# Layer 0 projects the raw x: the norm's gain moves into the weight split, its root into the results

## The chip, the cores and the metric

The kernel runs on one core of one Trainium2 chip. A time is the device time of one launch in microseconds (us); a kernel is timed several times and its median is compared. A profile is one further look at one execution: its span runs from the first to the last recorded instruction.

## The reference

Four residual layers, then a last RMSNorm, for 256 tokens of width 1024 in float32. Layer 0 and layer 3 are pooling layers, layer 1 is a gated DeltaNet, layer 2 an attention. Only the start of layer 0 and its pooling mixer matter here:

```python
def rmsnorm(x, g):
    y = xf * lax.rsqrt(jnp.mean(xf * xf, axis=-1, keepdims=True) + EPS)
    return (y * g.astype(jnp.float32)).astype(x.dtype)

def pool_mixer(h, w_in, w_grp, scale, w_out):        # h = rmsnorm(x, norm_g[0])
    u, gate = jnp.split(h @ w_in, 2, axis=-1)        # 1024 -> 2 x 2048
    ...                                              # windowed means of u, minus u, per group of 512
    p = jnp.einsum('bsgi,gio->bsgo', p, w_grp).reshape(B, S, POOL_WIDTH)
    y = p * scale * jax.nn.silu(gate)
    return y @ w_out
```

## The kernel before

Tokens lie in two tiles of 128 (`xs[0]`, `xs[1]`, 1024 columns each). A projection contracts over `k`, eight blocks of 128 channels (`KD`), into strips of 512 output columns (`CW`). Each float32 product is made of three matmuls on operands split in two parts, `hi` (rounded for TensorE) and `lo` (the rest): hi·hi, hi·lo, lo·hi. So every weight block of 128x512 that lands in a `raw` tile is split by `weights`: ScalarE writes `whi` (line 117), VectorE writes `wlo = raw - whi` (line 119). Nine such pairs can be held (`ring`, 9 buffers); a pair's buffers come free when the matmuls that read them have ended.

The normed input goes in as `hT`: the four 128x128 blocks of half a token tile are transposed on TensorE into a PSUM bank (`tp`, line 324), then split by ScalarE and VectorE (`split_out`, lines 196 and 201) into `hTh` and `hTl`.

The work of layer 0 in order: for the four groups `g` = 3, 2, 1, 0 a `gate` strip and a `pooled` strip (each 1024 x 512), with the group's own 512x512 product (`mixed`) one group behind; then `layer_out`. The first gate strip (`rows`, line 168) puts tokens on the output's partitions, 48 matmuls with 512 columns: 8 blocks x 2 token tiles x 3. The other seven strips (`chan=True`, lines 127 to 129) put channels on the partitions, 96 matmuls with 256 columns each. A gate strip's result is turned by ScalarE through Silu (line 421), a pooled strip's copied by ScalarE (line 429).

The start, before the change: both halves of `xs[0]` are loaded, the gain `norm_g[0]` is loaded as a tile broadcast over all 128 partitions (`gain_tile`, line 277), `part_done` takes the mean square of the rows (ScalarE, line 210), GpSimd its root (line 297), VectorE writes the normed `h` (line 304), and only then `h` is transposed. Loads of the second token tile stand behind those of four weight blocks. Meanwhile 24 transposes of the identity (line 271) are issued to TensorE, with no use for their result.

The order of instructions on each engine comes from a scheduler that runs over the whole program when it is built; `later(...)` holds instructions back behind named ones. All loads of x and of weights are issued by SyncE (SP) in one queue. Each engine runs its own instructions in order and waits by semaphores.

Of the kernel before, what the change touches and what calls it, by code (L numbers as in the profile page):

```python
# [8 lines left out]
F32 = mybir.dt.float32  # L9
# [3 lines left out]
AF = mybir.ActivationFunctionType  # L13
# [29 lines left out]
def trunk(ctx: ExitStack, tc: tile.TileContext, x, positions, norm_g, pool_w_in, pool_w_grp,  # L43
# [6 lines left out]
    WARM = 24  # L50
    FREE = 4
    EARLY = 6
    E0 = 2
    E1 = 4
# [27 lines left out]
    def bank(pool, name):  # L82
        return pool.tile([P, CW], F32, tag=name, name=name)
# [13 lines left out]
    def weights(src, n, cols, raw=None, pool=()):  # L97
# [12 lines left out]
        for k in range(n):  # L110
            v = raw[:, k * cols:(k + 1) * cols]
            lo = ring.tile([P, CW], F32R, tag="wlo", name="wlo")[:, :cols]
            hi = ring.tile([P, CW], F32R, tag="whi", name="whi")[:, :cols]
            held = held_back["free"] <= 0
            held_back["free"] -= 1
            with later(*(held_back["after"] if held else ())):
                a = nc.scalar.copy(hi, v)  # L117
                e = nc.gpsimd if k in pool else nc.vector
                b = e.tensor_tensor(out=lo, in0=v, in1=hi.bitcast(F32), op=ALU.subtract)  # L119
            parts.append((hi, lo))  # L120
# [10 lines left out]
    def project(src, ks, act, cols=CW, chan=False, tail=0, done=None, cuts=1,  # L131
                where="acc", pool=()):
# [9 lines left out]
        def unit(k0, n):  # L142
            return weights(src(k0, n), n, cols,
                           pool=[a for a in range(n) if (k0 + a) % KD in pool])
# [44 lines left out]
    def units(n):  # L189
        return [(k, KU) for k in range(0, n, KU)]  # L190
# [63 lines left out]
    def load_x(t):  # L254
        for c in range(2):
            sl = slice(c * CW, (c + 1) * CW)
            nc.sync.dma_start(out=xs[t][:, sl], in_=x[0, t * P:(t + 1) * P, sl])

    load_x(0)
# [9 lines left out]
    ps = bank(tps, "tp")  # L269
    for _ in range(WARM):  # L270
        nc.tensor.transpose(ps[:, :P], ident, ident)

    def gain_tile(row, between):
# [6 lines left out]
        return g  # L280

# [130 lines left out]
    def pool_layer(i, j, hT):  # L412
        yT = Split("yT", POOL_W // P)
        order = (3, 2, 1, 0)

        def gate(g):
            ks = [(k, 1) for k in range(KD)] if g == order[0] and i == 0 else units(KD)
            banks = project(cols_of(pool_w_in[j], POOL_W + g * CW), ks, hT, chan=g != order[0])
            gs = [worka("gs", CW) for _ in range(NT)]
            for t in range(NT):  # L420
                nc.scalar.activation(gs[t], banks[t], AF.Silu)
            return gs

        def pooled(g):
            w = WINDOWS[g]
            banks = project(cols_of(pool_w_in[j], g * CW), units(KD), hT, chan=True)
            u = big("u", 4, S)
            for b in range(2):
                nc.scalar.copy(u[:, 2 * b:2 * b + 2, :],  # L429
                               banks[b].rearrange("p (c s) -> p c s", c=2))  # L430
# [784 lines left out]
    def prefetch(k, pool=()):  # L1215
        ready.append(weights(first(k, 1), 1, CW, worka("raw", CW), pool))

    def start(t):
        with later(*held_back["after"], *[mark[e] for e in ("act", "dve") if t]):
            for a in range(0, D, CW):  # L1220
                part_done(t, a, CW, apart=True)
            for a in range(0, D, CW):
                if t:
                    nxt.begin(t, a)
            nxt.feed(t)

    held_back["free"] = 100
    nxt = LayerIn(0, lambda: prefetch(0, (0,)))
    for k in range(1, E0):
        prefetch(k)  # L1230
    start(0)
    held_back["free"] = 0
    for k in range(max(1, E0), E1):
        prefetch(k)
    load_x(1)
    start(1)
    for k in range(E1, EARLY):
        prefetch(k)
# [33 lines left out]
```

## Time and profile before

| what | value |
|---|---|
| median of 3 timed runs | 859.24 us (858.56, 859.24, 861.16) |
| span of the profiled execution | 858.3 us |
| time of the profiled execution outside of its span | not given; the timed runs lie 0.3 to 2.9 us above the span |
| granted TensorE clock, mean | 0.988 |
| TensorE busy, matmuls | 836.9 us (98%) |
| VectorE busy | 594.2 us (69%) |
| ScalarE busy | 490.2 us (57%) |
| TensorE busy, 0 to 18.57 us | 11.52 us |
| TensorE busy, 18.57 to 171 us (the rest of layer 0) | 152.43 us of 152.43 |

In a row of the timeline stand the start and the duration in us, the engine, the line, the operation, the tiles (written from read) and how often; the brackets at the end tell how long the engine had idled, and what ended it. In a row of the windows stand the stretch and its length, then for PE (matmuls), PEld (weight loads), DVE (VectorE), ACT (ScalarE) and POOL (GpSimd) the busy us and the instructions, then the clock granted to TensorE as a share of full speed, the busy share of the DMA engines and the GB/s they moved. A row of the groups gives line, engine, operation, tiles, shapes and count, then busy us and mean ns of one, then the idle time before. Matmuls are pipelined: the distance of their starts, not the duration of one, is what a stream of them costs.

### The profile page before, as it was taken

The numbers are of one execution on the slowest core, as the hardware profiler recorded it, in microseconds if no ns is written. First come the engines' busy times: TensorE is split into PE (matmuls) and PEld (weight loads), VectorE is DVE, ScalarE is ACT, GpSimd is POOL, SyncE is SP. The second block draws the span as 40 slices with busy tenths as digits, with TensorE's granted clock in tenths as the row PEclk, the third lists the DMA queues.
The fourth block names the chain that finished last, engine by engine and source line by source line (L and its number), as shares of the span: only waits on it lengthen the run. The fifth ranks groups of instructions, "written<-read, shape, count | busy, mean of one in ns | idle before, by whom it ended". The sixth has DMA issues, their size and how long they took to land.

```text
span 858.3 us, 16132 instructions
## 1 busy us (share of the span) xinstructions
PE 836.9 (98%) x5967; PEld 778.9 (91%) x5967; DVE 594.2 (69%) x1140; ACT 490.2 (57%) x1007; POOL 155.2 (18%) x295
## 2 busy tenths in 40 slices
PE   6999999999999989999999999999999999999996
PEld 5999998988999988788979998999989989999986
DVE  4689866556988976355577659678767668867852
ACT  5566564467855744355465654566555475555642
POOL 4000000233237980022212002000000210000012
PEclk8999999999999999899999999999999999999999
DMA  6766666646655554123547676743552546556551
GB/s 196 245 190 185 179 194 198 194 138 198 193 141 168 171 149 131 66 67 106 173 139 217 198 171 172 195 127 97 172 163 82 175 148 209 182 179 196 190 201 50
DMA packets 109239, 140.42 MB, mean 164 GB/s; under 512 B 21228, under 2 KB 51112, under 8 KB 109160
## 3 DMA queue, kind: packets, MB, share of 16 engines
q1 hardware_dynamic: 106800, 137.65, 53.1%
q0 software_dynamic: 528, 1.58, 0.7%
q8 instruction: 47, 0.77, 0.4%
q10 hardware_dynamic: 1832, 0.16, 0.2%
q14 instruction: 32, 0.26, 0.1%
HBM read 137.79 MB, written 1.58 MB: 162 GB/s over the span
## 4 chain that ended last, share of the span: by engine, by line
PE 82%; POOL 7%; DVE 5%; DMA 3%; issue 2%; ACT 1%; SPq 0%; POOLq 0%; ACTq 0%; DVEq 0%
PE acc L168 33%; PE acc L128 11%; PE acc L127 11%; PE acc L129 11%; POOL Tb L732 3%; POOL pr L728 2%; PE aux L127 2%; PE aux L128 2%; PE aux L129 2%; DVE wlo L119 1%; DMA gain<-in_norm_g_dram 1%; DVE cv L637 1%; DVE h L304 1%; PE aux L861 1%; DMA Gb<-d_g 1%
## 5 line engine op out<-in xcount | busy, mean ns | idle before, releaser
L119 DVE TENSOR_TENSOR wlo<-raw,whi 128x512 fp32r<-128x512 f32 (+1 forms) x493 | 342.5, 717 | 162.6 <-ACT whi L117 155.4
L117 ACT CAST whi<-raw 128x512 fp32r<-128x512 f32 (+1 forms) x508 | 301.8, 617 | 256.7 <-PE acc L168 100.4
L127 PE MATMUL acc<-hTh,whi 128*128 128x256 f32 x832 | 234.3, 282 | 1.2 <-DVE vc L637 1.2
L128 PE MATMUL acc<-hTl,whi 128*128 128x256 f32 x832 | 235.0, 283 | 0.0
L129 PE MATMUL acc<-hTh,wlo 128*128 128x256 f32 x832 | 233.8, 281 | 0.0
L127 PEld LDWEIGHTS acc<-hTh,whi 128*128 128x128 f32 x832 | 156.9, 189 | 1.8 <-DVE vc L637 1.4
L128 PEld LDWEIGHTS acc<-hTl,whi 128*128 128x128 f32 x832 | 156.9, 189 | 0.4
L129 PEld LDWEIGHTS acc<-hTh,wlo 128*128 128x128 f32 x832 | 156.8, 189 | 0.2
L168 PE MATMUL acc<-wlo,yTh 128*128 128x256 f32 (+1 forms) x384 | 116.5, 319 | 0.0
L168 PE MATMUL acc<-whi,yTh 128*128 128x256 f32 (+1 forms) x384 | 116.4, 323 | 0.0
L168 PE MATMUL acc<-whi,yTl 128*128 128x256 f32 (+1 forms) x384 | 92.7, 322 | 0.0
L168 PEld LDWEIGHTS acc<-wlo,yTh 128*128 128x128 f32 x384 | 72.1, 188 | 5.1
L168 PEld LDWEIGHTS acc<-whi,yTh 128*128 128x128 f32 x384 | 71.7, 188 | 5.2
L168 PEld LDWEIGHTS acc<-whi,yTl 128*128 128x128 f32 x384 | 63.2, 188 | 5.5
L292 POOL TENSOR_TENSOR hg<-x,gain 128x256 f32<-128x256 f32 x18 | 14.9, 834 | 259.1 <-DVE x L354 257.4
L168 PE MATMUL acc<-wlo,hTh 128*128 128x512 f32 (+1 forms) x144 | 56.3, 396 | 0.4 <-DVE wlo L119 0.2
L168 PE MATMUL acc<-whi,hTh 128*128 128x512 f32 (+1 forms) x144 | 55.6, 394 | 0.7 <-ACT hTh L196 0.7
L168 PE MATMUL acc<-whi,hTl 128*128 128x512 f32 (+1 forms) x144 | 45.7, 389 | 0.0
L435 POOL COPY win<-u 128x4 f32<-128x4 f32 x8 | 2.8, 355 | 177.2 <-ACT u L429 177.2
L168 PEld LDWEIGHTS acc<-whi,hTh 128*128 128x128 f32 x144 | 27.5, 191 | 6.8 <-ACT hTh L196 1.7
L168 PEld LDWEIGHTS acc<-wlo,hTh 128*128 128x128 f32 x144 | 27.3, 190 | 6.8 <-DVE wlo L119 1.7
L168 PEld LDWEIGHTS acc<-whi,hTl 128*128 128x128 f32 x144 | 26.8, 190 | 5.5
(339 smaller groups left out, 1444.5 us busy)
## 6 DMA issues: line engine op xcount, KB each, us to landing
raw<-in_pool_w_in_dram SPq DMA_DIRECT2D x60, 512.0 KB, 4.5
raw<-in_gdn_w_in_dram SPq DMA_DIRECT2D x48, 512.0 KB, 3.9
raw<-in_pool_w_out_dram SPq DMA_DIRECT2D x32, 512.0 KB, 4.2
raw<-in_mla_w_in_dram SPq DMA_DIRECT2D x24, 512.0 KB, 4.6
raw<-in_mla_w_uq_dram SPq DMA_DIRECT2D x36, 256.0 KB, 3.4
raw<-in_pool_w_grp_dram SPq DMA_DIRECT2D x16, 512.0 KB, 4.1
raw<-in_gdn_w_out_dram SPq DMA_DIRECT2D x16, 512.0 KB, 3.7
raw<-in_mla_w_ukv_dram SPq DMA_DIRECT2D x32, 256.0 KB, 3.3
```

What stands on the lines that cost most here:

```text
L117: a = nc.scalar.copy(hi, v)
L119: b = e.tensor_tensor(out=lo, in0=v, in1=hi.bitcast(F32), op=ALU.subtract)
L127: nc.tensor.matmul(o, lhsT=lhs[0], rhs=rhs[0], start=start, stop=False)
L128: nc.tensor.matmul(o, lhsT=lhs[0], rhs=rhs[1], start=False, stop=False)
L129: return nc.tensor.matmul(o, lhsT=lhs[1], rhs=rhs[0], start=False, stop=stop)
L168: nc.tensor.matmul(o, lhsT=act(k, t * P, P)[x], rhs=parts[j][z][:, sl], start=k == first and x == z == 0, stop=k == last and x == 1)
L292: nc.gpsimd.tensor_tensor(out=self.early[t, a], in0=xs[t][:, sl], in1=self.g[:, sl], op=ALU.mult)
L304: nc.vector.scalar_tensor_tensor(out=h[:, cut:], in0=xs[t][:, sl], scalar=r[:, 0:1], in1=self.g[:, sl], op0=ALU.mult, op1=ALU.mult)
L637: nc.vector.scalar_tensor_tensor(out=o[:, d:], in0=ps[:, :S - d], scalar=tp(3 - d, c), in1=o[:, d:], op0=ALU.mult, op1=ALU.add)
L728: nc.gpsimd.tensor_tensor(out=pv, op=ALU.mult, in0=Lb[:, r, r + 1:, None].to_broadcast([M * Q, n, c]), in1=Tb[:, r:r + 1, :c].to_broadcast ...
L732: mark["blocks"] = nc.gpsimd.tensor_tensor(out=tv, in0=tv, in1=pv, op=ALU.subtract).ins
L861: nc.tensor.matmul(ps[:, c], lhsT=U[0][:, h, :], rhs=vR[h // 2][:, 0, c * DV:(c + 1) * DV], start=True, stop=True)
```

## The change

Layer 0 no longer forms a normed `h`. It transposes and splits x itself, half a token tile at a time, as it lands (`First.feed`). The gain `norm_g[0]` is loaded as 8 rows of 128 by ScalarE's queue (`grow`), transposed to columns (`First.columns`), and multiplied into every weight block of layer 0's input projection when it is split: ScalarE's `hi` is now an activation with a per-partition scale, VectorE's `lo` a scalar_tensor_tensor. The root of the mean square is applied to the results: in the first gate strip as the per-partition scale of the Silu, in the other seven strips by a VectorE multiply with `rT`, the roots spread over all partitions (`First.scales`: two matmuls of a diagonal with ones, and a copy). There the ScalarE copy of a pooled strip is gone, and the Silu of a gate strip follows the multiply. Loads of x and weights alternate. Of TensorE's idle work, 5 and 2 matmuls of ones are left in place of the 24 transposes. Layers 1 to 3 and the last norm are as before.

```diff
-    WARM = 24
+    WARM = (5, 2)
...
+                if gain is None:
+                    a = nc.scalar.copy(hi, v)
+                    b = e.tensor_tensor(out=lo, in0=v, in1=hi.bitcast(F32), op=ALU.subtract)
+                else:
+                    g = gain[:, k:k + 1]
+                    a = nc.scalar.activation(hi, v, AF.Copy, scale=g)
+                    b = e.scalar_tensor_tensor(out=lo, in0=v, scalar=g, in1=hi.bitcast(F32),
+                                               op0=ALU.mult, op1=ALU.subtract)
...
-    load_x(0)
+    load_x(0, 0)
+    grow = small("grow", P, bufs=1)[:KD]
+    nc.scalar.dma_start(out=grow, in_=norm_g[0].rearrange("(k p) -> k p", p=P))
+    ones = const.tile([P, P], F32, name="ones")
+    nc.vector.memset(ones, 1.0)
...
-    ps = bank(tps, "tp")
-    for _ in range(WARM):
-        nc.tensor.transpose(ps[:, :P], ident, ident)
+
+    def warming(n):
+        ps = bank(tps, "tp")
+        for _ in range(n):
+            nc.tensor.matmul(ps[:, :P], lhsT=ones, rhs=ones, start=True, stop=True)
+
+    warming(WARM[0])
...
+    class First:
...
+        def columns(self):
+            ps = bank(tps, "tp")
+            nc.tensor.transpose(ps[:, :KD], grow, ident[:KD, :KD])
+            nc.vector.tensor_copy(self.gain, ps[:, :KD])
+
+        def feed(self, t, c):
+            ps = bank(tps, "tp")
+            for b in range(4):
+                a = c * CW + b * P
+                nc.tensor.transpose(ps[:, b * P:(b + 1) * P], xs[t][:, a:a + P], ident)
+            return split_out((ps.rearrange("p (b s) -> p b s", b=4),
+                              self.hT.many(4 * c, 4, t * P, P), None))
+
+        def scales(self):
+            ps = bank(aux, "aux")
+            for t in range(NT):
+                nc.gpsimd.tensor_tensor(out=self.r[t], in0=ms[t], in1=neghalf[:, :1], op=ALU.pow)
+                d = workb("diag", P)
+                nc.vector.tensor_scalar(d, ident, self.r[t], None, ALU.mult)
+                nc.tensor.matmul(ps[:, t * P:(t + 1) * P], lhsT=ones, rhs=d, start=True, stop=True)
+            nc.vector.tensor_copy(self.rT, ps[:, :S])
...
+        def scaled(o, ps):
+            nc.vector.tensor_tensor(
+                out=o, in0=ps.rearrange("p (c s) -> p c s", c=2), op=ALU.mult,
+                in1=lead.rT[:, None, :].to_broadcast([P, 2, S]))
...
-            for t in range(NT):
-                nc.scalar.activation(gs[t], banks[t], AF.Silu)
+            if lead and not chan:
+                lead.scales()
+            for t in range(NT):
+                if not lead:
+                    nc.scalar.activation(gs[t], banks[t], AF.Silu)
+                elif chan:
+                    scaled(gs[t].rearrange("p (c s) -> p c s", c=2), banks[t])
+                    nc.scalar.activation(gs[t], gs[t], AF.Silu)
+                else:
+                    nc.scalar.activation(gs[t], banks[t], AF.Silu, scale=lead.r[t])
...
             for b in range(2):
-                nc.scalar.copy(u[:, 2 * b:2 * b + 2, :],
-                               banks[b].rearrange("p (c s) -> p c s", c=2))
+                if lead:
+                    scaled(u[:, 2 * b:2 * b + 2, :], banks[b])
+                else:
+                    nc.scalar.copy(u[:, 2 * b:2 * b + 2, :],
+                                   banks[b].rearrange("p (c s) -> p c s", c=2))
...
+    nxt = First()
+    nxt.columns()
+    turn = nxt.feed(0, 0)
+    with later(*turn):
+        prefetch(0)
+        warming(WARM[1])
+        prefetch(1)
+    load_x(1, 0)
+    with later(mark["act"], mark["dve"]):
+        turn = nxt.feed(1, 0)
+    with later(*turn):
+        prefetch(2)
+        prefetch(3)
+        part_done(0, 0, CW, apart=True)
+    load_x(0, 1)
+    load_x(1, 1)
...
```

What moves is seen in the order in which the built programs hold their instructions. SyncE's queue at the start of the program, before (`x_93` and `x_94` are the two token tiles, `raw` the weight blocks):

```order
L257 DMA x_93<-in_x_dram 128x512 x2
L277 DMA gain<-in_norm_g_dram 128x512
L104 DMA raw<-in_pool_w_in_dram 128x512
L277 DMA gain<-in_norm_g_dram 128x512
L104 DMA raw<-in_pool_w_in_dram 128x512 x3
L257 DMA x_94<-in_x_dram 128x512 x2
```

and now:

```order
L260 DMA x_93<-in_x_dram 128x512
L101 DMA raw<-in_pool_w_in_dram 128x512
L260 DMA x_94<-in_x_dram 128x512
L101 DMA raw<-in_pool_w_in_dram 128x512
L260 DMA x_93<-in_x_dram 128x512
L101 DMA raw<-in_pool_w_in_dram 128x512
L260 DMA x_94<-in_x_dram 128x512
L101 DMA raw<-in_pool_w_in_dram 128x512
```

The two broadcast loads of the gain are gone from this queue, and the second token tile's first half stands third in place of eighth.

TensorE at the start of the program, before (`tp` are the transposes' banks, `acc` the sums of a strip):

```order
L271 MATMUL tp<-ident 128x128 x24
L324 MATMUL tp<-ident,h 128x128 x8
L168 MATMUL acc<-whi,hTh_168 128x512
L168 MATMUL acc<-wlo,hTh_168 128x512
L168 MATMUL acc<-whi,hTl_169 128x512
```

and now:

```order
L280 MATMUL tp<-ones 128x128 x5
L304 MATMUL tp<-ident,grow 128x8
L311 MATMUL tp<-ident,x_93 128x128 x4
L280 MATMUL tp<-ones 128x128 x2
L311 MATMUL tp<-ident,x_94 128x128 x4
L172 MATMUL acc<-whi,hTh_130 128x512
L311 MATMUL tp<-ident,x_93 128x128 x4
L172 MATMUL acc<-wlo,hTh_130 128x512
L172 MATMUL acc<-whi,hTl_131 128x512
```

The transposes read x, not `h`, four at a time, and stand behind that of `grow`; the first projections stand between them. TensorE's order is otherwise moved by a few rows within layer 0, and from the first rows of layer 0's output projection on it is the same, row for row; the other engines' orders differ no later.

VectorE near the end of the first strip with channels on the partitions, before:

```order
L392 COPY colsT<-tp 128x128
L119 TENSOR_TENSOR wlo<-raw,whi 128x512 x8
L436 TENSOR_TENSOR win<-u 128x4x255
L526 CAST bws<-bw 128x8x16
L119 TENSOR_TENSOR wlo<-raw,whi 128x512 x2
```

and now:

```order
L434 COPY colsT<-tp 128x128
L121 SCALAR_TENSOR_TENSOR wlo<-raw,gain_118,whi 128x512 x3
L459 TENSOR_TENSOR u<-acc,rT 128x512
L121 SCALAR_TENSOR_TENSOR wlo<-raw,gain_118,whi 128x512
L459 TENSOR_TENSOR u<-acc,rT 128x512
L121 SCALAR_TENSOR_TENSOR wlo<-raw,gain_118,whi 128x512
L588 CAST bws<-bw 128x8x16
```

VectorE now empties the strip's two banks (`u<-acc,rT`) among the weight splits of the strips to come.

69 lines of the change are left out of this document (32 added, 37 removed).

## The prediction

> **What bounds the kernel now.** I read the busy time by stretches first, then the chain of waits and the timeline of the start. The windows of the start, of the rest of layer 0 and of what follows:
>
> ```profile
> 0.00:18.57 18.57, 11.52 (x53) 9.62 (x53) 6.46 (x10) 9.28 (x20) 7.57 (x37) 0.82 0.70 226
> 18.57:171.00 152.43, 152.43 (x1138) 145.14 (x1138) 109.89 (x192) 87.67 (x153) 13.90 (x47) 1.00 0.64 194
> 171.00:858.30 687.30, 672.93 (x4780) 624.14 (x4778) 477.86 (x939) 393.25 (x835) 133.76 (x213) 0.99 0.52 155
> ```
>
> From 18.57 us to the end of layer 0 TensorE never idles. What brings its stream forward there moves the end by as much; what leaves the stream alone is worth nothing. So all hangs on how much projection is done when the stream closes up. The timeline of the start:
>
> ```profile
> 0.80 0.87 SPq L257 DMA_DIRECT2D x<-in_x_dram  x2
> 3.44 0.63 ACT L210 ACTIVATE junk<-x 128x512 f32<-128x512 f32 x1 [1.15 <-DMA x<-in_x_dram]
> 7.83 0.75 DVE L304 SCALAR_TENSOR_TENSOR h<-x,xr,gain 128x512 f32<-128x512 f32 x1 [7.83 <-DMA gain<-in_norm_g_dram]
> 8.64 1.11 PE L324 MATMUL tp<-ident,h 128*128 128x128 f32 x4 [2.41 <-DVE h L304]
> 13.50 0.63 PE L168 MATMUL acc<-whi,hTl 128*128 128x512 f32 x1
> 13.93 0.63 PE L168 MATMUL acc<-whi,hTh 128*128 128x512 f32 x1
> 17.48 1.09 PE L324 MATMUL tp<-ident,h 128*128 128x128 f32 x8 [0.70 <-ACT h L309]
> 18.38 0.99 PE L168 MATMUL acc<-whi,hTh 128*128 128x512 f32 x2
> ```
>
> The first half of x is there at 3.44, but VectorE waits for the broadcast gain until 7.83. The chain of waits has that load's second half until 10.06, and line 168's windows count what is done before the second token tile's norm is ready:
>
> ```profile
> 2.66 7.40 DMA gain<-in_norm_g_dram
> 61.59 5.60 PE acc L168 x24
> 12.40:16.80 4.40, 4.28 (x12) 3.14 (x12) 0.68 0.71 267
> ```
>
> That is 12 of the first gate strip's 48 matmuls. The other 36 start at 18.38; at 5.60/24 = 0.233 us each they are worth 8.40 us. So before, this strip is through, with no idle time after it, at 18.38 + 8.40 = **26.78 us**.
>
> **The change, part by part.** *When inputs land.* Half a token tile and a weight block, 256 KB each, alternate four times; then come pairs of blocks, 512 KB. The first half of x lands at 3.44 as before. The rate of the rest is bounded by two stretches in which the DMA engines were full with such loads:
>
> ```profile
> 2.50:3.00 0.50, 0.50 (x4) 0.50 (x3) 0.00 (x0) 0.00 (x0) 0.00 (x0) 1.00 0.97 311
> 10.00:10.50 0.50, 0.00 (x0) 0.00 (x0) 0.34 (x1) 0.00 (x0) 0.50 (x1) 0.50 1.07 410
> ```
>
> At 311 to 410 GB/s 256 KB takes 0.64 to 0.84 us; I take 0.75. The first weight block lands near 4.2, the second tile's x 4.9, weights 5.7, then 6.4, 7.2, 7.9, 8.7, and the pairs near 10.2 and 11.7. The two gain loads that held the chain are off this queue.
>
> *The splits.* The groups by form:
>
> ```profile
> L117 ACT CAST whi<-raw 128x512 fp32r<-128x512 f32 x500 | 298.3, 620 | 253.9 <-PE acc L168 98.8 <-PE acc L128 79.6 <-DMA raw<-in_pool_w_in_dram 21.1
> L309 ACT ACTIVATE h<-hg,xr 128x256 f32<-128x256 f32 x18 | 8.2, 502 | 4.4 <-POOL xr L297 4.4
> L196 ACT CAST yTh<-ym 128x256 fp32r<-128x256 f32 x16 | 6.5, 409 | 6.9 <-DVE ym L1197 6.7
> L196 ACT CAST hTh<-tp 128x512 fp32r<-128x512 f32 x16 | 9.3, 582 | 7.1 <-PE tp L324 6.8
> L210 ACT ACTIVATE junk<-x 128x512 f32<-128x512 f32 x12 | 7.6, 630 | 1.3 <-DMA x<-in_x_dram 1.1
> L210 ACT ACTIVATION_READ_ACCUMULATOR junk<-x 128x1 f32 x28 | 5.2, 186 | 0.0
> L119 DVE TENSOR_TENSOR wlo<-raw,whi 128x512 fp32r<-128x512 f32 x111 | 74.5, 693 | 38.0 <-ACT whi L117 37.6
> L458 DVE SCALAR_TENSOR_TENSOR y<-aux,colsT,gs 128x256 f32<-128x256 f32 x12 | 5.0, 477 | 0.0
> L354 DVE TENSOR_TENSOR x<-acc,x 128x256 f32<-128x256 f32 x16 | 6.7, 421 | 12.8 <-PE acc L168 12.8
> L201 DVE TENSOR_TENSOR hTl<-tp,hTh 128x512 fp32r<-128x512 f32 x16 | 11.0, 686 | 4.2 <-ACT hTh L196 4.2
> ```
>
> A per-partition scale costs ScalarE 502 - 409 = 0.09 us, so a scaled `whi` is put at 0.71. A scalar operand costs VectorE 477 - 421 = 0.06 us, so `wlo` is put at 0.75, which the row at 7.83 shows outright. A mean square takes ScalarE 0.63 + 0.19 = 0.82.
>
> *TensorE's start.* The transposes of the first half of x run 3.5 to 4.6 (1.11, row at 8.64, slow clock), two matmuls of ones to 5.05, the second tile's transposes to 6.15. What such a float32 matmul costs is bounded from the other end by this row (0.11 us each at full clock, doubled to 0.22 at half):
>
> ```profile
> 217.93 1.50 PE L690 MATMUL aux<-kqT 128*128 128x128 f32 x12
> ```
>
> ScalarE in its order: `hTh` to 5.2, `whi` to 5.9 and 6.6, `hTh` 7.2, `whi` 7.9, a mean square, `whi` 9.4, two `hTh` 10.6, `whi` 12.0, a mean square, `whi` 14.2; VectorE ends the eighth `wlo` near 15.1. TensorE: one projection at 5.9; transposes of the next half (lands 6.4) to 7.6; eight projections; the last four transposes; then 39 projections. At half clock the starts lie 13.93 - 13.50 = 0.43 apart. If full clock comes near 9.0: 3.3 projections to 9.0, 4.7 at 0.233 to 10.1, four transposes at full clock (1.09/2) to 10.65, 39 x 0.233 = 9.1, end **19.75**. The last twelve begin at 17.0, after every `wlo`: nothing waits. The two matmuls of `scales` add 0.22. Gain: 26.78 - 19.75 - 0.22 = **6.8 us**.
>
> *The roots.* The fourth mean square follows 12 `whi` and four `hTh` on ScalarE and ends near 18.7; GpSimd's two steps after it need under a microsecond. The strip's Silu and the second diagonal matmul stand behind 19.75, so cost nothing; were the root 2 us later, TensorE would wait about that, since the matmul of the diagonal stands inside the next strip's row.
>
> *The evictions.* Fourteen banks of seven strips are now multiplied by VectorE, eight ScalarE copies go. The rows, and VectorE's load where they fall:
>
> ```profile
> L465 DVE TENSOR_TENSOR y<-acc,gs 128x512 f32<-128x512 f32 x2 | 1.3, 678 | 0.0
> 30.00:130.00 100.00, 100.00 (x805) 97.91 (x804) 78.58 (x137) 60.84 (x103) 5.70 (x10) 1.00 0.64 191
> 50.00:100.00 50.00, 50.00 (x402) 48.90 (x401) 42.53 (x82) 31.27 (x55) 2.76 (x5) 1.00 0.66 195
> 70.00:80.00 10.00, 10.00 (x88) 10.00 (x87) 9.76 (x24) 7.34 (x14) 0.00 (x0) 1.00 0.62 162
> ```
>
> 14 x 0.68 = 9.5, and 48 splits x 0.06 = 2.9: VectorE comes to 78.6 + 12.4 = 91 of 100 us, in the densest half to 42.5 + 6.2 = 48.7 of 50. TensorE hides it, because the nine split pairs are about 9 x 6 x 0.233 = 12.6 us of its work. The fullest 10 us become about 11; that is 1 us late, taken from those 12.6. I count nothing, and up to 3 us if that cover is gone. An eviction waits for its strip's end with later `wlo` behind it, and TensorE waits for those; but these could not be written much sooner, as their ring places come free only as that strip is consumed.
>
> *The sum.* 858.3 - 6.8 = 851.5 of span. The median lies 0.94 above that span; with this added, **852.4 us**.
>
> **The rivals.** *The clock stays low.* The windows of the start in steps of 3.4 us:
>
> ```profile
> 4.90:8.30 3.40, 1.33 (x12) 1.09 (x10) 0.47 (x1) 0.10 (x2) 0.76 (x2) 1.00 0.81 211
> 8.30:11.70 3.40, 1.11 (x4) 0.71 (x4) 1.83 (x3) 1.54 (x3) 1.26 (x1) 0.51 1.02 379
> 11.70:15.10 3.40, 3.36 (x10) 2.88 (x11) 2.78 (x5) 2.39 (x6) 1.43 (x2) 0.50 1.00 373
> ```
>
> After a stretch with 1.33 us of work the clock was halved; after one with 3.36 it was full. Now the 24 transposes are gone, and TensorE is dense only from about 5. If full clock comes at 11.7: eight projections at 0.43 end at 11.0, transposes 11.9, 39 x 0.233 give 21.0, gain 5.5, **853.7**. At 15.1: transposes 12.1, seven more at 0.43, 32 x 0.233 give 22.6, gain 4.0, **855.2**. At 4.9: one projection at 5.9, transposes 6.95, then 47 x 0.233 and 0.55, end 18.5, gain 8.1, 851.1: the floor. (The Trainium skill, "TensorE: Matmul & The Clock Gate", section on the HAM clock gate, says that the gate watches free-running windows of about 3.4 us, and wants one busy throughout for full clock. By that rule, the trace agrees; dense work from 5.0 would bring it between 8.4 and 11.8, so 852.2 to 853.7.)
>
> *The small gain row comes late.* TensorE's x transposes stand behind that of `grow`, and every `whi` needs it. Loads of this kind on ScalarE's queue took:
>
> ```profile
> rows<-in_pool_scale_dram ACTq DMA_DIRECT2D x2, 8.0 KB, 4.6
> ```
>
> That was beside a full weight queue; x itself took 3.44 - 0.8 = 2.6 at an empty one, and `grow` is issued at the same empty moment. If it takes 4.6 it lands at 5.4, transposes start 2 us later, all the rest with them: gain 4.8, **854.4**; with full clock at 15.1 besides, some 857.
>
> *Slower: VectorE becomes layer 0's bound.* The place is 30 to 130 us, the price that of a three-operand split. The same form has also been slow, when GpSimd worked beside it:
>
> ```profile
> L304 DVE SCALAR_TENSOR_TENSOR h<-x,xr,gain 128x512 f32<-128x512 f32 x2 | 2.3, 1138 | 9.4 <-DMA gain<-in_norm_g_dram 9.4
> ```
>
> At 1.14 us, 48 splits add (1.14 - 0.69) x 48 = 21.6, evictions 9.5: 78.6 + 31.1 = 109.7, 10 us more than TensorE's 100, and the end 10 - 6.8 later: **862**. It decides from 0.69 + (21.4 - 9.5 + 6.8)/48 = 1.08 us a split. Against it: GpSimd is busy 5.7 of those 100 us, and the first of the two took 0.75.
>
> *The shift is eaten in layer 0*, by the 3 us above: 855.4. *No change at all*, if the start were no limit: excluded by the first table, unless the root's chain holds TensorE for as long as the norm did; 859.
>
> **How the numbers follow.** Forecast 0.60 (full clock at 4.9 to 10); clock later 0.15; gain row late 0.10; eaten 0.07; VectorE the bound 0.05; no change 0.03. About 0.3%, 2.6 us, can be told from no change, so faster means under 856.7: 0.60 + 0.15 + 0.08 + 0.05 = 0.88, taken as 0.87; same 0.07; slower 0.06. The range goes from the floor of 851.1 less some noise, 850.5, to 857.0, which holds the clock and the gain row together.
>
> **What would show it.** Right: x transposes from about 3.5, no idle time of TensorE over a microsecond after 7.6, the gate strip through near 20, and from 30 to 130 us TensorE full with VectorE near 91 of 100. Wrong: a wait of the transposes for `grow`; a clock of 0.5 beyond 10; TensorE waiting for `wlo`, for `rT`'s diagonal or for a bank held by an eviction; splits on VectorE above 0.9 us; or idle time in layers 1 to 3 beyond the 687.30 - 672.93 = 14.4 us of before.

## The result and the profile after

| | before | after |
|---|---|---|
| median | 859.22 us (858.56 to 861.16, 4 runs) | 854.60 us (854.41 to 855.05, 4 runs) |
| span of the profiled execution | 858.3 us | 852.7 us |
| time of the profiled execution | not given | 854.42 us |
| first `x<-acc` of layer 0's output on VectorE | 151.7 us | 145.8 us |
| VectorE busy | 594.2 us | 602.2 us |

The ratio is 0.9945, with an interval of 0.9931 to 0.9959: 4.6 us faster (3.5 to 5.9), where 6.8 was forecast. The last row but one is used as a mark below: VectorE's first addition of a finished piece of layer 0 to x. It comes well before 300 us, where most of the spread from one execution to the next begins (shown at the end), so it tells differences of the start far more sharply than the whole time does.

The windows of the changed kernel that answer to those shown of before:

```profile
0.00:18.57 18.57, 16.16 (x69) 13.54 (x70) 9.96 (x16) 11.93 (x22) 5.90 (x59) 1.00 0.71 231
18.57:165.00 146.43, 146.43 (x1116) 140.54 (x1115) 115.29 (x201) 84.05 (x140) 15.19 (x21) 1.00 0.66 198
30.00:130.00 100.00, 100.00 (x801) 97.73 (x800) 88.45 (x152) 59.27 (x95) 8.95 (x10) 1.00 0.64 192
165.00:852.70 687.70, 672.74 (x4781) 624.27 (x4779) 476.92 (x939) 392.74 (x835) 134.84 (x213) 0.99 0.52 155
```

The clock of 1.00 in the first row does not tell the speed of the start: four transposes take 1.11 us in the rows from 3.75 to 8.36 below, and 0.60 us at 11.38, so the matmuls ran at half speed until about 9.7 us. Below, the speed of the start is read from such durations.

TensorE is again without a gap from 18.57 us to the end of layer 0, now with VectorE at 88.45 of 100 us. After layer 0 the idle time is 687.70 - 672.74 = 15.0 us, where it was 14.4. So the whole difference is made ahead of 18.57 us. The mark of the end of layer 0, from the rows of the tile x, first of before, then of after (the two times at the end are the first and the last start):

```profile
L354 DVE TENSOR_TENSOR x<-acc,x x6: 409/425/693, 151.7 to 175.6; 128x256 f32<-128x256 f32 x4, 128x512 f32<-128x512 f32 x2
```
```profile
L396 DVE TENSOR_TENSOR x<-acc,x x6: 410/425/691, 145.8 to 169.7; 128x256 f32<-128x256 f32 x4, 128x512 f32<-128x512 f32 x2
```

Layer 0 ends 5.9 us earlier. Before has one profile alone, so this is the difference of two executions. The timeline of TensorE at the start of the changed kernel, with the last matmuls of the first gate strip:

```profile
3.75 1.11 PE L311 MATMUL tp<-ident,x 128*128 128x128 f32 x4
4.66 1.06 PE L280 MATMUL tp<-ones 128*128 128x128 f32 x4
7.01 1.12 PE L311 MATMUL tp<-ident,x 128*128 128x128 f32 x4 [1.29 <-DMA x<-in_x_dram]
7.78 0.78 PE L172 MATMUL acc<-whi,hTh 128*128 128x512 f32 x1
8.36 1.11 PE L311 MATMUL tp<-ident,x 128*128 128x128 f32 x4
9.12 0.77 PE L172 MATMUL acc<-wlo,hTh 128*128 128x512 f32 x1
9.69 0.45 PE L172 MATMUL acc<-whi,hTl 128*128 128x512 f32 x1
...
20.93 0.62 PE L172 MATMUL acc<-whi,hTl 128*128 128x512 f32 x2
21.38 0.28 PE L132 MATMUL acc<-hTh,wlo 128*128 128x256 f32 x1
```

The strip gives way to the next one at 21.38. Four matmuls of that next strip lie inside it (0.47 us), so it is through after some 20.9 us of its own work, 5.9 earlier than the 26.78 of before: the same 5.9 that the end of layer 0 moved. The row at 7.01 holds the main miss: the second tile's x was awaited for 1.29 us and landed at 7.0. SyncE had issued that load third:

```profile
1.72 0.42 SPq L260 DMA_DIRECT2D x<-in_x_dram  x1
```
```profile
0.00:7.00 7.00, 4.60 (x19) 4.06 (x19) 1.70 (x4) 2.69 (x4) 4.62 (x55) 1.00 0.68 201
```

So these 256 KB took 5.3 us to land, while seven further loads were issued behind them. The bytes were not missing: 201 GB/s over 7 us are 1.41 MB, 5.4 loads of 256 KB, when only three loads were through. So parts of later loads were moved before the last part of the third. By the times from issue to landing, the second load was through at 4.1 us, the third at 7.0 and the seventh at 9.6: one late load, and then one every 0.65 us.

### The profile page after: what moved, and what is told of

It is laid out like the page before. It is cut to its first block, busy times and chain, and to the rows that moved or that the text cites. A ratio compares the mean times of both kernels' runs of the same rounds, so it can differ in the third digit from the quotient of the medians.

```text
span 852.7 us, 16120 instructions
## 1 busy us (share of the span) xinstructions
PE 835.3 (98%) x5962; PEld 778.4 (91%) x5962; DVE 602.2 (71%) x1156; ACT 488.7 (57%) x997; POOL 155.9 (18%) x292
## 4 chain that ended last, share of the span: by engine, by line
PE 68%; POOL 6%; DVE 2%; issue 1%; DMA 1%; ACT 1%; SPq 0%; POOLq 0%; ACTq 0%
PE acc L172 29%; PE acc L130 9%; PE acc L131 9%; PE acc L132 9%; POOL Tb L794 2%; POOL pr L790 2%; PE aux L130 1%; PE aux L131 1%; PE aux L132 1%; PE aux L752 1%; PE aux L923 1%; DMA Lb<-d_l 1%; PE tp L1246 1%; DVE h L346 1%; DVE wlo L117 1%
## 5 line engine op out<-in xcount | busy, mean ns | idle before, releaser
L117 DVE TENSOR_TENSOR wlo<-raw,whi 128x512 fp32r<-128x512 f32 (+1 forms) x430 | 299.0, 719 | 145.7 <-ACT whi L116 143.6
L116 ACT CAST whi<-raw 128x512 fp32r<-128x512 f32 (+1 forms) x444 | 263.2, 617 | 222.6 <-PE acc L172 98.4
L120 ACT ACTIVATE whi<-raw,gain 128x512 fp32r<-128x512 f32 x64 | 43.1, 719 | 30.2 <-DMA raw<-in_pool_w_in_dram 22.9
L121 DVE SCALAR_TENSOR_TENSOR wlo<-raw,gain,whi 128x512 fp32r<-128x512 f32 x64 | 46.8, 746 | 12.6 <-ACT whi L120 12.4
```

The lines of the kernel that those rows point to most:

```text
L120: a = nc.scalar.activation(hi, v, AF.Copy, scale=g)
L121: b = e.scalar_tensor_tensor(out=lo, in0=v, scalar=g, in1=hi.bitcast(F32), op0=ALU.mult, op1=ALU.subtract)
```

## The experiments

Each was timed beside the kernel before on the same chip, and has one profile. On these chips the time of one and the same kernel varies by some 7 us from run to run (the kernel before: 855.96 to 863.13 in 33 runs), so medians are given with their ratio, and the mark of layer 0's end decides on questions of the start.

### The changed kernel once more

Edit: none. This ran as the measure for later variants.

> The changed kernel once more, untouched, as the measure for the three beside it. Every theory expects the start of the first run's profile: last matmuls of the first gate strip ending at 21.4 us, VectorE's first x<-acc of layer 0 at 145.8 us, no wait of TensorE between 18.6 us and there; the total 854 to 856, less sure, since the stretches at half clock in the middle of the program fall differently in each execution.

Measured: 855.38 us (853.0 to 858.32), ratio 0.9945 [0.9924, 0.9967]. The mark:

```profile
L396 DVE TENSOR_TENSOR x<-acc,x x6: 409/424/691, 145.9 to 169.8; 128x256 f32<-128x256 f32 x4, 128x512 f32<-128x512 f32 x2
```

In these two executions the mark repeats within 0.1 us, though the medians differ by 0.8. The gain repeats too.

### Three loads in flight

Edit: the loads of the start are issued in the change's order, but each waits, by a one-column write of GpSimd into its target, until the load three places ahead has landed.

```diff
+    ORDER = ['x00', 'w0', 'x10', 'w1', 'x01', 'w2', 'x11', 'w3', 'w4', 'w5']
+    WINDOW = 3
...
+        if WINDOW and len(landed) >= WINDOW:
+            nc.gpsimd.tensor_copy(dst[:, :1], landed[len(landed) - WINDOW][:, :1])
```

> Same order of loads as in the changed kernel, but each of the first ten waits until the third before it has landed (GpSimd copies one column of it into the next target), so only three are under way at a time. Theory (loads under way share the DMA engines, so each lands late because of those issued after it): the second token tile's x lands near 5 us in place of 7.0, the first projection starts near 6.3 in place of 7.8, and the span is 0.8 to 1.5 us shorter than the changed kernel's 852.7, if the engines don't run dry. Rival (loads land one after the other in order of issue, and the slow stretch of 3.5 to 5 us at 180 GB/s alone made x late): x of the second tile still lands at 7.0, later loads later, span 852.7 to 854.

Measured: 855.76 us, ratio 0.995 [0.9932, 0.9968]. From the timeline and the waits of TensorE, and the mark:

```profile
5.58 0.66 PE L344 MATMUL tp<-ident,x 128*128 128x128 f32 x4
7.72 0.63 PE L344 MATMUL tp<-ident,x 128*128 128x128 f32 x4 [1.06 <-DMA x<-in_x_dram]
```
```profile
PE acc L178 <- ACT ph L537: 1.4, 1, 1.4
```
```profile
L425 DVE TENSOR_TENSOR x<-acc,x x6: 412/424/692, 147.2 to 171.0; 128x256 f32<-128x256 f32 x4, 128x512 f32<-128x512 f32 x2
```

The second tile's x is there by 5.58, at least 1.4 us earlier than in the first profile of the change. That fewer loads beside it did this is not shown: with the same order and all loads in flight, TensorE's wait for this x ended at 5.83 us in the run without idle matmuls (shown below), at 7.04 with doubled evictions, and here in the second run of the change and with tripled evictions:

```profile
6.68 1.12 PE L311 MATMUL tp<-ident,x 128*128 128x128 f32 x4 [0.97 <-DMA x<-in_x_dram]
```
```profile
6.49 0.66 PE L311 MATMUL tp<-ident,x 128*128 128x128 f32 x4 [1.10 <-DMA x<-in_x_dram]
```

So its landing differs by over a microsecond from one execution to the next, and 5.58 is only 0.25 us ahead of the earliest of these. The theory's shorter span was not seen either (855.5 us). What lands early is paid for by what lands after it: the next half of x is awaited until 7.72, a later weight split for 0.4 us, and the strip gives way at 21.24 against 21.38. Holding the loads back gains nothing. The mark is even 1.4 us later, by a wait that the change does not have: TensorE waits for `ph`, the split of the pooled result, at 56.8 us. VectorE works 18.87 and 19.40 us of the two 20 us from 40 and from 60 there; its slack is small. In the change, which has no such wait, it works 18.97 and 19.69, so its load alone does not explain the wait.

### The loads in the order of before

Edit: `ORDER = ['x00', 'x01', 'w0', 'w1', 'w2', 'w3', 'x10', 'x11', 'w4', 'w5']`, `WINDOW = 0`: everything of the change but the alternation of the loads.

> The changed kernel with x and weights loaded in the order of before: both halves of the first token tile, four weight blocks, then the second tile. Theory (TensorE has the first tile's twelve projections to do until the second tile lands, and what counts is when it is dense): second tile's x lands near 11, first projection near 6.5, span within 1 us of 852.7. Rival (the alternation is what brings the gain): TensorE idles several us before the second tile lands, span 855 to 857.

Measured: 855.69 us, ratio 0.997 [0.9951, 0.9988]. The longest wait of TensorE ahead of the end of layer 0, and the mark:

```profile
PE acc L178 <- ACT whi L124: 1.4, 1, 1.4
```
```profile
L425 DVE TENSOR_TENSOR x<-acc,x x6: 411/425/693, 146.9 to 170.8; 128x256 f32<-128x256 f32 x4, 128x512 f32<-128x512 f32 x2
```

By these two executions the alternation is worth 146.9 - 145.8 = 1.1 us. Their clocks differ, though: here the matmuls ran at full speed from about 4.9 us and at half from 8.3 to 11.7, in the changed kernel at half up to 9.7.

### No idle matmuls

Edit: `WARM = (0, 0)` in place of `(5, 2)`.

> The changed kernel without its 5 and 2 idle matmuls of ones. Theory (full clock needs a stretch of some 3.4 us with TensorE busy, and the idle work gives it about 9.6): without it full clock comes at 11 or later, some 6 more projections at 0.43 in place of 0.233, span 1 to 2 us longer, 853.7 to 854.7. Rival (dense work from 7 us on sets the clock): no change, 852.5 to 853.

Measured: 855.31 us, ratio 0.9957 [0.9943, 0.9971], mark at 145.9, strip giving way at 21.24. Full speed came near 10.3 us, as in the second run of the change (9.7 in the first). The timeline:

```profile
2.32 0.24 PE L304 MATMUL tp<-ident,grow 8*128 8x8 f32 x1 [2.32 <-DMA grow<-in_norm_g_dram]
5.83 1.12 PE L311 MATMUL tp<-ident,x 128*128 128x128 f32 x4 [1.32 <-DMA x<-in_x_dram]
```

So these seven matmuls are not shown to help or to harm. In this execution the second tile's x was there at 5.83 us, 1.2 us earlier than in the change, and that may hide a loss. The first row also gives the landing of the small gain load, issued at 0.80: 2.32 at the latest, 1.5 us, and not the 4.6 of the rival in the prediction.

### Before, without the load of the broadcast gain

Edit, on the kernel before; the product leaves out `norm_g[0]`:

```diff
+        if between:
+            nc.vector.memset(g, 1.0)
+            between()
+            return g
```

> The kernel before, with layer 0's gain tile set to ones by VectorE and not loaded; this leaves the gain norm_g[0] out of the result. Theory (the second tile's x, mean square and root close the stream, the first tile's gain only moves work that is done in time anyway): twelve projections start about 3 us earlier, the stream closes at 17 to 18 in place of 18.38, span 857 to 858.3 against 858.3. Rival (the broadcast gain load is what the change saves): most of the 5.6 us, span 853 to 854.5.

Measured: 857.74 us, ratio 0.9984 [0.9967, 1.0]. The projections begin at 8.03, and the mark:

```profile
8.03 0.50 PE L168 MATMUL acc<-whi,hTh 128*128 128x512 f32 x1
```
```profile
L358 DVE TENSOR_TENSOR x<-acc,x x6: 411/424/691, 148.8 to 172.6; 128x256 f32<-128x256 f32 x4, 128x512 f32<-128x512 f32 x2
```

This is 2.9 us earlier than before, and 3.0 later than the change. Both spans expected are missed (855.7 was measured): in these profiles the late gain was half of what the change removed. The other half would be the chain of the norm itself (mean square, root, multiply, for both tiles) and the second tile's late loads; they were not taken apart. Two loads fewer also bring the second tile's x forward: GpSimd takes it up at 8.97 us, and at 12.81 before. How much of that is the landing of single executions is not known, since there is one profile of each. In the total only some 1 us of the 2.9 is seen, a quarter of the change's 4.6 and at the edge of what can be told.

### Every eviction twice, and three times

Edit: each of the 14 scaled evictions is repeated; the same values are written again.

```diff
-            nc.vector.tensor_tensor(
-                out=o, in0=ps.rearrange("p (c s) -> p c s", c=2), op=ALU.mult,
-                in1=lead.rT[:, None, :].to_broadcast([P, 2, S]))
+            for _ in range(2):
+                nc.vector.tensor_tensor(
+                    out=o, in0=ps.rearrange("p (c s) -> p c s", c=2), op=ALU.mult,
+                    in1=lead.rT[:, None, :].to_broadcast([P, 2, S]))
```

> Each of the 14 scaled evictions of layer 0 is done twice on VectorE (the same values are written again), 9.5 us more of VectorE there: 88.5 of 100 us in the stretch from 30 to 130 us would become about 98. The theory of the prediction (VectorE's work is covered by the ring of pairs that is filled ahead): TensorE waits 1 us at most, layer 0 ends at most 1 us later (first x<-acc by 146.8). The rival (VectorE is at the edge already: 19.69 of 20 us in the stretch from 60 to 80 us, and the result of the pooling is ready only 2.5 us before TensorE takes it): the 9.5 us come in part ahead of that result, TensorE waits for ph or for a pair in 40 to 80 us, and layer 0 ends 3 to 6 us later.

> The same with three of each, 19 us more of VectorE: 107 of 100 us wanted in the stretch from 30 to 130 us. With a cover of 12.6 us (nine pairs ahead) as the prediction had it, layer 0 ends 0 to 7 us later. With VectorE at the edge from the start it ends 9.5 us later than with two of each, and the waits of TensorE are for ph and for split pairs. Neither theory has a place for more than 19 us.

Measured: twice 857.62 us, ratio 0.997 [0.9952, 0.9987]; three times 873.11 us, ratio 1.0146 [1.0125, 1.0166]; the untouched kernel on that chip 855.38. One group of VectorE, the waits of TensorE and the mark with two of each:

```profile
L460 DVE TENSOR_TENSOR u<-acc,rT 128x512 f32<-128x512 f32 x16 | 10.6, 680 | 0.0
```
```profile
PE tp L311 <- DMA x<-in_x_dram: 2.1, 2, 1.7
PE tp L433 <- DMA rows<-in_gdn_norm_g_dram: 0.8, 1, 0.8
PE acc L172 <- ACT ph L509: 0.4, 1, 0.4
```
```profile
L396 DVE TENSOR_TENSOR x<-acc,x x6: 410/424/692, 148.8 to 172.2; 128x256 f32<-128x256 f32 x4, 128x512 f32<-128x512 f32 x2
```

The mark is 2.9 us later than in the untouched kernel, near the lower end of the rival's 3 to 6, but not for its reason alone. In this execution x was awaited longer and the granted clock was half from 8.2 to 11.6, so that the first matmul of the roots' diagonal stands 0.8 us later; 0.8 us is a wait for a row of parameters; 0.4 us is the wait for `ph` that the rival named. Some 0.9 us are not accounted for. So VectorE's extra work cost 0.4 to 1.3 us here: the cover is there, but it is nearly used up. VectorE was busy for 91.89 of the 100 us from 30 to 130, not the 98 of the expectation, since a part of its work moved behind them. With three of each it is gone:

```profile
61.08 0.80 PE L172 MATMUL acc<-whi,ph 128*128 128x512 f32 x1 [4.62 <-ACT ph L509]
```
```profile
58.00:66.00 8.00, 4.92 (x15) 4.15 (x16) 7.45 (x11) 2.15 (x3) 0.00 (x0) 0.60 0.36 119
```
```profile
L396 DVE TENSOR_TENSOR x<-acc,x x6: 414/425/692, 158.1 to 181.5; 128x256 f32<-128x256 f32 x4, 128x512 f32<-128x512 f32 x2
```
```profile
PE aux L883 <- DMA T<-d_t: 9.4, 1, 9.4
```

TensorE waits 4.62 us for `ph`, and the granted clock then falls to half (0.60 over those 8 us). Layer 0 ends 158.1 - 145.9 = 12.2 us later than in the untouched kernel on that chip. That is 8.2 us of waits of TensorE after 20 us (4.6 for `ph`, 1.7 for a `whi`, 1.7 for a row of parameters, 0.2 for `pl`, the `lo` part of the pooled result) and some 5 us of lost clock (0.95 over the 100 us from 30), less a first strip that gave way 1.2 us earlier (20.20 against 21.42). That it ends 9.3 us later than with two of each, near the 9.5 of the third evictions, is chance: there the strip gave way only at 22.18. The total rises by 17.7 us over the untouched kernel, more than the 12.2 of layer 0. The last row, from the waits of layer 1, has the larger part of the rest: TensorE waits 9.4 us, until 326 us, for a round trip of T, a tile of layer 1, through device memory. In the untouched kernel other work of TensorE stood beside that round trip; whether the late chain or another order of instructions took that work away was not tested.

### The loads in pairs, twice

Edit: `ORDER = ['x00', 'x10', 'w0', 'w1', 'x01', 'x11', 'w2', 'w3', 'w4', 'w5']`, `WINDOW = 0`: both tiles' halves of x ahead of two weight blocks.

> The loads in another order, all issued at once as in the change: both tiles' first halves of x, two weight tiles, both second halves, then the rest of the weights. If the loads share the engines and the last byte counts, the second tile's x lands near 5.8 us in place of 7.0, the first weights near 7.1 in place of 6.0, the first projection starts 7.5 to 8.2, and the end of the first gate strip stays within 0.6 us of 21.4. If loads landed one after another, as the prediction had it, the first weights would land 0.75 us later than in the change, and the strip would end 0.7 us later.

> The loads in pairs, untouched, a second time and on the same chip as the run beside it. If the earlier end of layer 0 belongs to this order, the first x<-acc of VectorE stands at 144.4 to 145.4 again and full speed comes by 7 us; if it was that execution's luck with the clock, it stands at 145.6 or later. Total expected 0.992 to 0.995 of the kernel before.

Measured: 854.59 us, ratio 0.9934 [0.9913, 0.9955]; the second time 852.98 us, ratio 0.9915 [0.989, 0.9939]. The timeline of the first, and the marks of the first and the second:

```profile
5.51 0.66 PE L344 MATMUL tp<-ident,x 128*128 128x128 f32 x4
6.59 0.50 PE L178 MATMUL acc<-whi,hTh 128*128 128x512 f32 x1 [0.43 <-ACT whi L124]
```
```profile
L425 DVE TENSOR_TENSOR x<-acc,x x6: 408/424/692, 144.9 to 168.7; 128x256 f32<-128x256 f32 x4, 128x512 f32<-128x512 f32 x2
```
```profile
L425 DVE TENSOR_TENSOR x<-acc,x x6: 410/425/692, 144.8 to 168.7; 128x256 f32<-128x256 f32 x4, 128x512 f32<-128x512 f32 x2
```

Both theories of the first expectation were wrong in the same direction. The first projection starts at 6.59, not after 7.5, and the strip ends at 19.1 (here with none of the next strip's matmuls inside), 1.8 us ahead of the change's 20.9; behind it TensorE waits 0.7 us for a row of parameters, and 1.0 us is left at the end of layer 0. In the second execution the strip ends at 19.9, that wait is absent, and the mark is the same within 0.1 us. The second expectation's first theory held at the mark (144.8); the total came just below its 0.992. TensorE has no gap of over half a microsecond from 1.1 to 7.6 us in the first of these executions, and its matmuls are at full speed from 5.5 us on (4 transposes in 0.66 us, not 1.11), in the second from about 6.6; in the change from 9.7.

### The gap filled with idle work

Edit: `WARM = (5, 5)`: three more matmuls of ones behind the first transposes, in the stretch where the change waits for x.

> The change with five matmuls of ones in place of two behind the first transposes (three more, some 1.3 us at half speed), so that the idle time of about 1.3 us in which TensorE waits for the second tile's x is filled with idle work. TensorE also does the first projection ahead of that tile's transposes. One theory: full speed comes at 5.5 us with the loads in pairs and only at 9.7 in the change because of that idle time; then full speed comes by 7.5 here, the first gate strip ends about 1 us earlier (near 20.4 with its four interleaved matmuls, against 21.4) and layer 0 ends near 144.9 (first x<-acc of VectorE) against 145.8. The rival: the gain of the pairs came from x landing earlier; then nothing moves here, 145.6 to 146.2.

Measured, on the same chip as the second run of the pairs: 852.95 us, ratio 0.9915 [0.9893, 0.9938]. The timeline and the mark:

```profile
4.66 2.34 PE L280 MATMUL tp<-ones 128*128 128x128 f32 x10
7.50 0.66 PE L311 MATMUL tp<-ident,x 128*128 128x128 f32 x4
8.95 0.51 PE L172 MATMUL acc<-whi,hTh 128*128 128x512 f32 x1 [0.31 <-ACT whi L120]
```
```profile
L396 DVE TENSOR_TENSOR x<-acc,x x6: 409/424/691, 145.5 to 169.4; 128x256 f32<-128x256 f32 x4, 128x512 f32<-128x512 f32 x2
```

Full speed is there by 7.5, as the first theory wanted, 2.2 us earlier than in the change. But the strip gives way at 21.0 against 21.38, and the mark moves by 0.3, nearer to the rival's 145.6 than to 144.9: with a faster TensorE the weights come late next (the wait of 0.31 at 8.95). So of the 1.0 us of the pairs some 0.3 can be the clock. The rest may be that x and weights land in the order in which they are used; that was not tested apart, and in this execution the second tile's x was taken up only at 7.50.

### The pairs, with the rows of parameters loaded early

Edit: the five small loads into `rows` are issued right after ScalarE's table load at the start, in place of 20 to 23 us.

> The loads in pairs as in the run before, and the five small loads of parameters (rows, 32 KB at most together, whose transposed tile TensorE waited 0.7 us for at 27 us there) issued right after the table load of ScalarE at the start, in place of 20 to 23 us. If that wait was due to their late issue, it is gone and layer 0 ends 0.7 us earlier than with the pairs alone: first x<-acc of VectorE at 144.2 us against 144.9 there and 145.9 in the change. The rival: the five issues, 0.3 us each on ScalarE, delay its first split at 4.9 us or slow the first loads of x, the strip ends later by up to 1.5 us and layer 0 ends at 144.9 to 146.4. The total is expected 0.5 to 1.7 us below the change (852.5 to 855), which is about the spread of a median here, so the end of layer 0 decides.

Measured: 854.94 us, ratio 0.9932 [0.9912, 0.9952]. The wait for the rows is gone, yet the mark is later than with the pairs alone. The scheduler moved other instructions with them. The timeline's two new waits, and the mark:

```profile
14.42 0.74 PE L178 MATMUL acc<-whi,hTh 128*128 128x512 f32 x2 [0.61 <-ACT whi L124]
65.51 0.44 PE L563 MATMUL tp<-ident,y 128*128 128x128 f32 x2 [1.00 <-DVE y L557]
```
```profile
L439 DVE TENSOR_TENSOR x<-acc,x x6: 411/424/691, 146.6 to 170.4; 128x256 f32<-128x256 f32 x4, 128x512 f32<-128x512 f32 x2
```

The rival was nearer. The first projection was not delayed by more than 0.14 us (6.73), but SyncE issued its third weight block at 5.89 us, in the first run of the pairs at 3.60; a weight pair came 0.6 us late, the strip gave way 1.6 us later (20.66), and the mark lies just past the rival's 146.4. VectorE's `y`, 1.0 us late, neither side had. In the second run of the pairs the wait for the rows was absent without any edit. So this edit is not shown to help.

No variant is shown to beat the change in the whole time: the pairs and the filled gap have the lower ratios, but their intervals overlap with the change's. In layer 0 the pairs are 1.0 us better.

## Why the prediction was right, and where not

The median of 854.6 lies in the range, and the way of the gain is the forecast one: the start alone, 5.9 us of layer 0, all the way to its end. The median alone would not tell this, since the rivals' 854.4 (gain row late) and 855.2 (clock later still) fit it better than 852.4; the traces do. The misses are of size.

**When inputs land** is the step that failed. It let 256 KB land every 0.75 us, one load after another: the second tile's x at 4.9, the next half at 6.4. They were there at 7.0 and 8.36 or a little before. The rate was hardly lower than assumed: 5.4 loads' worth had been moved by 7.0, where the forecast has 5.7. What failed is the 0.75 us from the second load to the third: it was 2.9 us, while parts of later loads were moved, and the loads behind it came about as much later. Why the third load is so late, and was awaited until anything from 5.83 to 7.04 us in different executions, is open. In the sum this is the first projection at 7.78 (forecast 5.9) and the strip of eight projections from 9.12 (7.6).

**TensorE's start.** Full speed was forecast near 9.0 and came near 9.7. Strip through: 20.9 in place of 19.75. With 0.22 for the roots' matmuls that is 5.7 us, and the mark moved by 5.9; forecast 6.8. A float32 matmul of ones was put at 0.22 us; it measured 0.43 at half speed, as two matmuls of 0.21 in the profile (five in the program are ten there, 2.50 us). This cost nothing, since TensorE waited for x behind them.

**The splits and the evictions** were right to a few per cent. The groups of the changed kernel, VectorE then ScalarE:

```profile
L121 DVE SCALAR_TENSOR_TENSOR wlo<-raw,gain,whi 128x512 fp32r<-128x512 f32 x55 | 40.3, 745 | 9.8 <-ACT whi L120 9.8
L459 DVE TENSOR_TENSOR u<-acc,rT 128x512 f32<-128x512 f32 x8 | 5.4, 683 | 0.0
```
```profile
L120 ACT ACTIVATE whi<-raw,gain 128x512 fp32r<-128x512 f32 x54 | 36.3, 719 | 28.6 <-DMA raw<-in_pool_w_in_dram 21.3 <-PE acc L132 2.8 <-PE acc L131 2.5
```

VectorE came to 88.45 of 100 us, forecast 91. That it is hidden was right as well. The reason given, 12.6 us of pairs split ahead, was too kind: what decides is the pooled result `ph`, which in the change is ready at 53.1 and used at 55.6. 9.5 us more of VectorE used that slack up, and 19 us more cost 12.2 us in layer 0, some 5 of them by the clock that fell behind the waits. So the slower rival, VectorE as the bound, had the right place; its price was not reached, since no split came near the 1.08 us from which it decides.

**The roots** cost nothing, as forecast: TensorE waits for none of their work.

**The rivals of the start.** The gain row was not late (2.32 at the latest). The clock was between the forecast and the first rival. The Trainium skill, "TensorE: Matmul & The Clock Gate", section on the HAM clock gate, has full clock come after a window of about 3.4 us that was busy throughout, with windows that run freely. The trace agrees: full speed came at 5.5 to 7.5 us in the runs where TensorE had no gap of over half a microsecond between 1.1 us and then, and near 10 in those with a gap of 0.8 to 1.3 us ahead of it. It does not agree to the letter: 3.4 us before the change's 9.7 is 6.3, and TensorE waited until 7.01. In the order of before, in three in flight and in the doubled and tripled evictions the matmuls at 4.7 to 5.6 were at full speed already; where a window begins, no run here shows.

**The sum.** The gain was mis-sized by 0.9 us. A second term is the 0.94 added to the span: the 33 runs of the kernel before in the first set of experiments lie 1.76 us above their spans, and those of the changed kernel 1.7 to 2.0. So the profiled execution of before took about 860.1 by estimate and lay 0.8 above its median, and the right addition was about 1.8. With both, 858.3 - 5.9 + 1.8 = 854.2; measured 854.42 for the execution profiled and 854.6 for the median.

*From 5.9 to 5.6 of span.* The end of layer 0 moved by 5.9 us, the span by 5.6. One place where the two executions differ is in layer 1, before's row first:

```profile
305.76 0.69 PE L677 MATMUL tp<-ident,kqT 128*128 128x128 f32 x2 [2.41 <-ACT kqT L671]
```
```profile
300.50 0.69 PE L739 MATMUL tp<-ident,kqT 128*128 128x128 f32 x2 [4.41 <-ACT kqT L733]
```

The lead is 5.3 us there, behind a wait that is 2.0 us longer. But this wait has one of two lengths in every profile here, 2.4 or 4.4 us, for variants of both kernels (except three evictions, whose wait stands elsewhere), so it is not the change's. What decides between them is open. The idle time of 15.0 us behind layer 0, 0.6 beyond the 14.4 that the prediction named as a limit, is less than these two waits differ by.

*From 5.6 of span to 4.6 of the medians* is only partly settled. The 0.8 by which before's profiled execution lay above its median is most of it. Its one profile had the granted clock at half from 8.4 to 15 us, where the changed kernel's matmuls ran at half speed up to 9.7; what that cost, and how often the executions of before have it, the runs don't tell.

## What to carry to other kernels

Do not count a load as landed when its own bytes have had their time at full rate: here the third of several loads issued close together landed when 5.4 loads' worth of bytes had been moved, and its landing differed by over a microsecond between executions. Order the first loads as they are used, and give such an early landing a range. When an engine is given work "under cover", look for the one result that the bound engine takes with the least slack, not for the mean share: here 88 us of 100 cost nothing, 9.5 us more cost 0.4 to 1.3, and 19 us more cost twelve. And measure an edit of the start by a mark soon after it, before other parts of the program add their own spread.

## What the runs showed of the hardware beside that

**Half clock comes in whole steps.** Two windows of after and two of before, each around a stretch of half clock (the third figure from the end is the mean granted clock):

```profile
299.00:304.00 5.00, 3.50 (x19) 3.51 (x20) 2.98 (x6) 3.18 (x7) 4.59 (x9) 0.66 0.22 63
347.00:355.00 8.00, 7.38 (x30) 6.22 (x31) 1.25 (x2) 1.78 (x5) 0.00 (x0) 0.57 0.00 1
```
```profile
305.00:309.00 4.00, 3.24 (x16) 3.24 (x17) 2.75 (x5) 3.18 (x7) 3.75 (x7) 0.57 0.45 141
353.00:360.00 7.00, 7.00 (x29) 5.82 (x30) 0.68 (x1) 1.68 (x4) 0.00 (x0) 0.51 0.00 0
```

The clock lost is (1 - 0.66) x 5 = 1.7 us, (1 - 0.57) x 8 = 3.4, (1 - 0.57) x 4 = 1.7 and (1 - 0.51) x 7 = 3.4: one step of 1.7 us or two, that is, stretches of 3.4 or 6.8 us at half. Between 286 and 386 us all thirteen profiles lose a whole number of such steps: two (3.4 us) in four of them, three in four, four in two, five in two, six with three evictions. At the start, after the first full speed: two steps in before from 8.4 us, one with the loads in before's order and one with doubled evictions from 8.2 to 8.3, none in the other ten. The Trainium skill, "TensorE: Matmul & The Clock Gate", section on the HAM clock gate, gives a window of 3413 ns; the trace agrees, with stretches of one or more such windows. The stretches of layer 1 begin in or soon after a gap of TensorE, though not every gap brings one: the wait for kqT above, and two waits of 0.67 and 0.79 us near 345 to 353 us. The same page, section "Why this matters for your kernels", warns of idle gaps of over about 3 us; here gaps of 2.4 us, and of 0.67 and 0.79 us among small matmuls, stand ahead of such stretches too. The stretch at 60 us with three evictions stands behind its wait of 4.62.

This is most of the spread of the whole time. The time from the mark to the end of the span is 703.6 to 713.5 us over these profiles; with the clock lost from 286 to 386 us taken off, it is 700.0 to 703.3. For an edit worth 1 us, a step more or less in one execution hides it.

**A dip of the loads' rate.** The DMA engines move 176 to 225 GB/s between 3.5 and 5.0 us in the changed kernel, where they moved 344 in the half microsecond ahead and 336 in the one behind, with several loads in flight. Before has a dip at the same place. Its cause was not tested.
